# Sparse attention's small matmuls on all 128 rows, with rows of zeros; the sum of squares of the compressed keys as one column

## The chip, the cores and the metric

The kernel runs on one core of one Trainium2 chip. A core has a matrix engine, TensorE (PE), that multiplies a stationary 128x128 array of weights by columns that stream through it and adds into PSUM banks; VectorE (DVE), ScalarE (ACT) and GpSimd (POOL) for everything else; and a queue of transfers issued by SyncE (SP). The metric is the device time of one execution in microseconds (us), lower is better.

## The reference, cut to what matters

Two blocks of two layers each over 256 tokens of width 1024. The change lies in the mixer of the first block, which runs twice (layers 0 and 1). Its sparse attention has 6 heads of 64 in two groups of three; a group shares its keys and values. Three branches are added with gates: compressed, selected and window. With 4 blocks of 64 keys and up to 16 selected, selection takes all that are causal.

```python
k_cmp = rms_norm(compress(kv[0, 0], 0), k_gain[0])     # 15 blocks of 32 tokens, two groups
v_cmp = compress(kv[0, 1], 1)                          # gelu(flat @ cmp_w1[j]) @ cmp_w2[j]
s_c = einsum('bghqd,bgnd->bghqn', qb, k_cmp) + bias_c
o_c = einsum('bghqn,bgnd->bghqd', masked_softmax(s_c, ...), v_cmp)
s_s = einsum('bghqd,bgqkd->bghqk', qb, ks) + bias_s    # selected keys
s_w = einsum('bghqd,bgkd->bghqk', qb, kw) + bias_w     # window keys
return g[..., 0:1] * o_c + g[..., 1:2] * o_s + g[..., 2:3] * o_w
sv = einsum('gts,bcsgd->bctgd', ws * causal, v) + b.T  # spatial gating, also in the mixer
```

## The kernel before, in words

Every large product with weights is made from two halves: a piece of 128x1024 weights is loaded (`raw`, 4 buffers, on SP), ScalarE rounds it to a high half `wh` (line 243), VectorE makes the rest `wl` (line 246), and TensorE adds three products of halves (`mm3`, line 269 records all of `mm1`). Those streams fill most of TensorE's time: `mm<-xx,wh`, `mm<-xx,wl` and so on. A matmul on plain F32 tiles is two passes in the trace; one on F32R tiles is one pass.

In `first_mixer` (twice) the order of each engine's instructions is set when the kernel is built: a list scheduler takes the code in program order, follows the tiles' dependencies and puts other matmuls where one would wait. Each engine then runs its list strictly in order.

What the change touches there:

- `qs`, `ks`, `kl` (lines 688 to 742): queries and keys of the two groups in high and low halves. `qs[:, e]` holds, for group e, the high half of the query on that group's 64 rows and its low half on the other 64. `ks[:, g]` holds the high half of group g's keys on both row halves; so one matmul of 128 rows makes high x high + low x high. `kl` holds the low half of the keys, both groups in one tile, each on its 64 rows, and the second matmul reads those 64 rows alone (line 829 by its code): high x low. Each runs per query tile tt with 2 x 128 or 2 x 256 columns (selected and window keys side by side), per half and per i: 4 x `ks` and 4 x `kl` for each call of `weights(i)`, i from 0 to 2.
- the compressed keys (lines 786 to 815): `gk` and `gv` come out of a gelu; `w2` (64 rows) makes from `gk` the keys and from `gv` the values, three times over, on 96 rows of the bank `kp`. ScalarE squares the keys (`ksq`, 64x32), a matmul with `ones` sums them to 32 rows of `st`, GpSimd raises that to the power -1/2 (`kr`), a matmul with the unit matrix spreads `kr` over all rows (`kb`), and VectorE multiplies (`kcb`). `vblk` (96 rows) is the values masked per group.
- `values(i)`: transposes the weights `z` of the heads (line 856), copies them (`pT`, ScalarE, line 859), multiplies them by the values `vt` (outputs on 64 rows each) and adds the compressed branch: `vblk` and `pcT`, 32 rows per i.
- the spatial gating: `pair` (2 rows) times `gb` (2 rows) puts the bias in the bank, and `vs` by `ws` is added.

`t` is a rotating set of six buffers of 128x256, `z` one of four, `wk` four PSUM banks. SP carries all loads in one list; a load that waits holds those behind it.

Of the kernel before, what the change touches and what calls it, by code (L numbers as in the profile page):

```python
# [1892 lines left out]
```

## Time and profile before

| | us |
|---|---|
| median of 3 runs (1279.09 to 1291.28) | 1288.11 |
| the profiled execution | 1287.02 |
| its span, first to last instruction | 1285.0 |
| TensorE busy | 1258.6 (98%) |
| VectorE busy | 1025.6 (80%) |
| ScalarE busy | 755.3 (59%) |
| GpSimd busy | 35.7 (3%) |

Rows of the timeline give the start, the duration and the instruction; runs of alike instructions are one row with a count (x2), whose duration is that of all of them together. Matmuls overlap in the array, so the distance from one start to the next is what one of them costs, and the duration is longer. In `64*128 64x256` the matmul uses 64 rows and 128 columns of the array, and 256 columns stream through. In square brackets stands what the engine waited for. The granted clock (PEclk) is 1.00 for 2.4 GHz and 0.50 for 1.2 GHz.

### The profile page before, as it was taken

Reading aid. Unit: us, or ns where it says so; the run is one execution under the profiler, and the core shown is the slowest. Engines: PE = TensorE matmul, PEld = TensorE weight load, DVE = VectorE, ACT = ScalarE, POOL = GpSimd, SP = SyncE. Lnnn points to the kernel's source line nnn. Section 1 sums busy time; section 2 is a strip of 40 time slices with the busy share of each in tenths; the row PEclk is TensorE's granted clock in tenths of the full one; section 3 lists DMA queues with packets and bytes.
Section 4 is the critical chain, followed back from the end, with each engine's and each line's share of the span. In section 5 each row is a group of like instructions: output and inputs, shape, how many; then the busy total and the mean of one; then the engine's idle time right before and its main releaser. Section 6 shows DMA issues by size and latency. Waiting matters only on the chain.

```text
span 1285.0 us, 22329 instructions
## 1 busy us (share of the span) xinstructions
PE 1258.6 (98%) x8335; PEld 1125.8 (88%) x8335; DVE 1025.6 (80%) x2294; ACT 755.3 (59%) x1388; POOL 35.7 (3%) x37
## 2 busy tenths in 40 slices
PE   7999999999999999999999999999999999999997
PEld 7887988888998799888889999888888989888886
DVE  6776697776777678998999984899988876999863
ACT  6467376555564846655465553677654565766652
POOL 0000100000010010000000000000000000000000
PEclk9999999999998999999999998999999999999998
DMA  8614456656652346665547242565656443565561
GB/s 285 215 57 133 146 171 191 196 179 187 202 178 72 105 139 214 199 188 184 166 134 240 71 160 60 176 188 189 191 182 193 154 148 116 180 213 187 181 190 34
DMA packets 63313, 211.83 MB, mean 165 GB/s; under 512 B 7992, under 2 KB 10981, under 8 KB 62693
## 3 DMA queue, kind: packets, MB, share of 16 engines
q1 hardware_dynamic: 63204, 210.41, 51.4%
q8 instruction: 65, 1.06, 0.4%
q14 instruction: 44, 0.35, 0.1%
HBM read 209.33 MB, written 1.06 MB: 164 GB/s over the span
## 4 chain that ended last, share of the span: by engine, by line
PE 86%; DVE 7%; ACT 2%; DMA 2%; issue 2%; POOL 0%; SPq 0%; POOLq 0%; DVEq 0%; ACTq 0%
PE mm L269 47%; PE wk L269 37%; DVE wl L246 2%; DMA raw<-weights 1%; ACT wh L243 1%; PE wk L856 1%; DMA z<-bias_line 1%; DMA x<-xt 0%; DVE xx L397 0%; DVE ma L1416 0%; DVE x L345 0%; ACT ks L740 0%; DVE mb L1410 0%; DVE Es L1302 0%; DVE Ec L1301 0%
## 5 line engine op out<-in xcount | busy, mean ns | idle before, releaser
L243 ACT ACTIVATE wh<-raw 128x1024 fp32r<-128x1024 f32 (+3 forms) x394 | 404.9, 1031 | 358.3 <-PE mm L269 164.6
L246 DVE TENSOR_TENSOR wl<-raw,wh 128x512 fp32r<-128x512 f32 (+3 forms) x666 | 500.0, 763 | 141.3 <-ACT wh L243 136.1
L269 PE MATMUL mm<-xx,wh 128*128 128x256 f32 (+1 forms) x1760 | 443.0, 328 | 0.3 <-DVE xx L397 0.3
L269 PE MATMUL mm<-xx,wl 128*128 128x256 f32 x1232 | 348.4, 283 | 1.0 <-DVE wl L246 1.0
L269 PEld LDWEIGHTS mm<-xx,wh 128*128 128x128 f32 x1760 | 297.1, 190 | 31.6 <-issue 2.4
L269 PE MATMUL wk<-xx,wh 128*128 128x512 f32 x704 | 247.6, 392 | 2.5 <-DVE xx L397 2.5
L269 PEld LDWEIGHTS mm<-xx,wl 128*128 128x128 f32 x1232 | 234.3, 190 | 2.0 <-DVE wl L246 1.2
L269 PE MATMUL wk<-xx,wl 128*128 128x256 f32 x704 | 198.5, 282 | 0.0
L269 PEld LDWEIGHTS wk<-xx,wh 128*128 128x128 f32 x704 | 132.2, 188 | 30.5 <-DVE xx L397 1.7
L269 PEld LDWEIGHTS wk<-xx,wl 128*128 128x128 f32 x704 | 133.0, 189 | 0.2
L269 PE MATMUL wk<-aa,wh 128*128 128x512 f32 x352 | 123.0, 392 | 0.0
L269 PE MATMUL mm<-aa,wh 128*128 128x512 f32 x352 | 122.9, 392 | 0.0
L269 PE MATMUL wk<-aa,wl 128*128 128x256 f32 x352 | 98.7, 280 | 0.3 <-DVE wl L246 0.3
L269 PE MATMUL mm<-aa,wl 128*128 128x256 f32 x352 | 98.6, 280 | 0.0
L269 PEld LDWEIGHTS mm<-aa,wh 128*128 128x128 f32 x352 | 66.1, 188 | 14.4
L269 PEld LDWEIGHTS wk<-aa,wh 128*128 128x128 f32 x352 | 66.1, 188 | 14.4
L269 PEld LDWEIGHTS wk<-aa,wl 128*128 128x128 f32 x352 | 66.2, 188 | 0.8 <-DVE wl L246 0.7
L269 PEld LDWEIGHTS mm<-aa,wl 128*128 128x128 f32 x352 | 66.2, 188 | 0.0
L269 PE MATMUL mm<-wh,xx 128*128 128x274 f32 (+3 forms) x224 | 56.0, 331 | 7.4 <-ACT wh L243 7.4
L322 ACT ACTIVATE aa<-a 128x256 fp32r<-128x256 f32 x88 | 35.9, 412 | 23.1 <-DVE a L499 23.1
L269 PEld LDWEIGHTS mm<-wh,xx 128*128 128x128 f32 x224 | 40.0, 199 | 10.4 <-ACT wh L243 7.4
L496 DVE SCALAR_TENSOR_TENSOR e<-gu,par,e 128x255 f32<-128x255 f32 (+1 forms) x88 | 41.3, 475 | 0.0
(476 smaller groups left out, 1779.1 us busy)
## 6 DMA issues: line engine op xcount, KB each, us to landing
raw<-weights SPq DMA_DIRECT2D x344, 512.0 KB, 3.7
raw<-weights SPq DMA_DIRECT2D x46, 384.0 KB, 3.2
h<-w SPq DMA_DIRECT2D x2, 1024.0 KB, 4.8
raw<-weights SPq DMA_DIRECT2D x4, 411.0 KB, 3.9
k_decay<-k_decay SPq DMA_DIRECT2D x1, 1152.0 KB, 7.7
x<-xt SPq DMA_DIRECT2D x4, 256.0 KB, 6.3
h<-s5c SPq DMA_DIRECT2D x1, 1024.0 KB
z<-bias_line SPq DMA_DIRECT2D x2, 384.0 KB, 5.4
```

The lines of the kernel that those rows point to most:

```text
L243: nc.scalar.activation(h[:, :n], r[:, :n], AF.Copy)
L246: self.last_low = nc.vector.tensor_sub(l[:, q], r[:, q], h[:, q].bitcast(F32))
L269: return self.nc.tensor.matmul(out, l, r, start=start, stop=stop, skip_group_check=True)
L322: self.nc.scalar.activation(h, src, AF.Copy)
L496: v.scalar_tensor_tensor(e[:, d:], gu[:, 0, :T - d], col(2 - d), e[:, d:], op0=OP.mult, op1=OP.add)
L856: nc.tensor.transpose(pt[:, blk * 128:blk * 128 + 128], zs[half][:, br, blk * 128:blk * 128 + 128], s.ident)
```

## The change

`kl` gets a dimension for the group; GpSimd clears the rows that are not that group's, once per layer, and the second score matmul reads all 128 rows of `qs` and `kl`. `gk` and `gv` move into one tile `gkv` of 128 rows whose lower half is cleared, and `w2` gets 64 rows of zeros. The matmul for the keys now takes all four of its column blocks (`gk` and three times `gv`). `ksq` squares all 128x128 of it, and the sum over 128 rows counts each square twice, as the keys stand twice in `w2`, hence 1/128 in place of 1/64; it comes out for 128 rows, of which the spread reads 32 through the unit matrix. `vblk` gets one 96x128 block per i, made by a product with the new constant `pick`, which is 1 on the 16 rows of that i and group; the matmul reads 96 rows. `pair` and `gb` get 128 rows with zeros below the second; `gb` moves into one of the `t` buffers, cleared by GpSimd just before its load, and the load is issued later in the program. `u2` takes the tile `turn`, whose use has ended, in place of its own.

```diff
@@ constants
+    pick = np.zeros((128, 3, 2), f)
+    for i in range(3):
+        for g in range(2):
+            pick[32 * i + 16 * g:32 * i + 16 * g + 16, i, g] = 1
+    c["pick"] = pick.reshape(128, 6)
-    pair = np.zeros((2, 128), f)
+    pair = np.zeros((128, 128), f)
@@ first_consts
-    for n in ("m32", "valid", "pair", "tri", "decay"):
+    for n in ("m32", "valid", "pair", "tri", "decay", "pick"):
@@ first_mixer
-    kl = P.tile([128, 2, T], F32R, name="kl")
+    kl = P.tile([128, 2, 2, T], F32R, name="kl")
+    nc.gpsimd.memset(kl[64:128, 0].bitcast(F32), 0.0)
+    nc.gpsimd.memset(kl[0:64, 1].bitcast(F32), 0.0)
...
-                v.tensor_sub(kl[rows[g], i], k[rows[g]], ks[rows[g], g, i].bitcast(F32))
+                v.tensor_sub(kl[rows[g], g, i], k[rows[g]], ks[rows[g], g, i].bitcast(F32))
...
-    w2 = P.tile([64, 192], F32, name="w2")
+    w2 = P.tile([128, 192], F32, name="w2")
...
-    gk = P.tile([64, 32], F32, name="gk")
-    gv = P.tile([64, 3, 32], F32, name="gv")
+    gkv = P.tile([128, 4, 32], F32, name="gk")
+    nc.gpsimd.memset(gkv[64:128], 0.0)
+    gk, gv = gkv[:, 0], gkv[:, 1:4]
...
-    s.mm1(kp[:, 0:32], w2[:, 0:128], gk)
-    s.mm1(kp[0:96, 64:128], gv.rearrange("p i n -> p (i n)"), w2[:, 128:192])
+    s.mm1(kp[:, 0:128], w2[:, 0:128], gkv.rearrange("p i n -> p (i n)"))
+    s.mm1(kp[0:96, 128:192], gv.rearrange("p i n -> p (i n)"), w2[:, 128:192])
...
-    sq = P.tile([64, 32], F32, name="ksq")
-    act(sq, kp[0:64, 0:32], AF.Square)
+    sq = P.tile([128, 128], F32, name="ksq")
+    act(sq, kp[:, 0:128], AF.Square)
...
-    for g in range(2):
-        v.tensor_scalar(vblk[:, g * 64:g * 64 + 64], kp[0:96, 64:128], s.c["cols"][0:96, 4 + g:5 + g], None, op0=OP.mult)
+    vblk = P.tile([96, 3, 2, 64], F32, name="vblk")
+    for i in range(3):
+        v.tensor_mul(vblk[:, i], kp[0:96, None, 128:192].to_broadcast([96, 2, 64]),
+                     s.c["pick"][0:96, 2 * i:2 * i + 2, None].to_broadcast([96, 2, 64]))
...
-    s.mm1(st[0:32, 0:1], sq, s.ones[0:64, 0:1])
+    s.mm1(st[:, 0:1], sq, s.ones[:, 0:1])
...
-    s.mm1(kb[:, 0:32], kr.to_broadcast([32, 128]), s.ident[0:32, 0:32])
+    s.mm1(kb[:, 0:32], kr.to_broadcast([128, 128]), s.ident[:, 0:32])
...
-                s.mm1(S[:, :2 * n], q[r], kl[r, :, :n], False, True)
+                s.mm1(S[:, :2 * n], q, kl[:, half, :, :n], False, True)
...
-        y = s.mm1(o[:, 0:T], vblk[q, :], pcT[q, :], False, True)
+        y = s.mm1(o[:, 0:T], vblk[:, i].rearrange("p a b -> p (a b)"), pcT, False, True)
...
-    gb = P.tile([2, 2, 128], F32, name="gb")
-    s.dma(gb, s.ext(f"gb{l}", ...))
...
-    u2 = P.tile([128, 2, T], F32, name="u2")
+    u2 = turn
...
+    gb = tmp().rearrange("p (a b) -> p a b", a=2)
+    nc.gpsimd.memset(gb, 0.0)
+    s.dma(gb[0:2], s.ext(f"gb{l}", ...))
...
-        f = s.mm1(o[:, 0:T], s.c["pair"], gb[:, i, None, :].to_broadcast([2, 2, 128]), True, False)
+        f = s.mm1(o[:, 0:T], s.c["pair"], gb[:, i, None, :].to_broadcast([128, 2, 128]), True, False)
```

The scheduler orders anew what follows. On TensorE, at the first scores of layer 0 (`kr` is the reciprocal root of the compressed keys, `kcb` the scaled compressed keys), before:

```order
L269 MATMUL wk<-k_ident,kr 128x32
L269 MATMUL wk<-ks,qs 128x256
L269 MATMUL wk<-kl,qs 128x256
L269 MATMUL wk<-ks,qs 128x512
L269 MATMUL wk<-kl,qs 128x512
L269 MATMUL wk<-ks,qs 128x256
L269 MATMUL wk<-kl,qs 128x256
L269 MATMUL wk<-ks,qs 128x512
L269 MATMUL wk<-kl,qs 128x512
L269 MATMUL wk<-kcb,qh 128x32 x6
```

and in the changed kernel:

```order
L275 MATMUL wk<-k_ident,kr 128x32
L275 MATMUL wk<-ks,qs 128x256
L275 MATMUL wk<-kl,qs 128x256
L275 MATMUL wk<-ks,qs 128x512
L275 MATMUL wk<-kl,qs 128x512
L275 MATMUL wk<-ks,qs 128x256
L275 MATMUL wk<-kl,qs 128x256
L275 MATMUL mm<-xx,wl 128x256
L275 MATMUL mm<-wh,xx 128x384
L275 MATMUL mm<-wl,xx 128x384
L275 MATMUL wk<-ks,qs 128x512
L275 MATMUL wk<-kl,qs 128x512
L275 MATMUL wk<-kcb,qh 128x32 x6
```

Three matmuls of the stream stand between the third and the fourth pair. On TensorE in layer 1, around the matmul that reads `gk`, before:

```order
L269 MATMUL mm<-xx,wh 128x256
L269 MATMUL wk<-gk,w_4170 128x32
L269 MATMUL wk<-w_4170,gv 96x64
L269 MATMUL mm<-xx,wh 128x256
L269 MATMUL mm<-xx,wl 128x256
L269 MATMUL mm<-xx,wh 128x256
L269 MATMUL wk<-ones,ksq 32x1
```

and now:

```order
L275 MATMUL mm<-xx,wh 128x256 x2
L275 MATMUL wk<-gk,w_4177 128x128
L275 MATMUL wk<-w_4177,gk 96x64
L275 MATMUL mm<-xx,wl 128x256
L275 MATMUL mm<-xx,wh 128x256 x2
L275 MATMUL mm<-xx,wl 128x256
L275 MATMUL wk<-ones,ksq 128x1
```

One stream matmul more stands ahead of `gk`, one more ahead of `ksq`, and three more (10 in place of 7) between `ksq` and `kr`. On GpSimd in layer 0 (`rrr` is the reciprocal root of a retention head pair, `t` here is `gb`):

```order
L360 TENSOR_TENSOR rrr<-rvv,mhalf 128x4
L1029 MEMSET t 128x256
L360 TENSOR_TENSOR rrr<-rvv,mhalf 128x4
L360 TENSOR_TENSOR r_1532<-v_1531,mhalf 128x8
L360 TENSOR_TENSOR rrr<-rvv,mhalf 128x4
```

The memset is new between the first two. On SP in layer 0 the load of `gb` stood right behind that of `ws`, and now:

```order
L180 DMA ws<-ws 128x512
L180 DMA raw<-weights 128x1024 x15
L180 DMA t<-gb 2x256
L180 DMA raw<-weights 128x1024 x44
```

It has moved behind 15 pieces of weights.

## Rows read from the trace of the kernel before

**Rows 1.** The page, part 1: busy time and share of the span
```profile
PE 1258.6 (98%) x8335; PEld 1125.8 (88%) x8335; DVE 1025.6 (80%) x2294; ACT 755.3 (59%) x1388; POOL 35.7 (3%) x37
```

**Rows 2.** Waits of TensorE: total us, times, longest us
```profile
PE wk L269 <- DMA z<-bias_line: 2.6, 2, 2.0
...
PE wk L269 <- issue: 1.5, 2, 1.2
```

**Rows 3.** Timeline of TensorE, layer 1: start us, us, instruction, [idle before]
```profile
393.24 0.38 PE L269 MATMUL wk<-gk,w 64*128 64x32 f32 x2 [1.18 <-issue]
...
395.79 0.58 PE L269 MATMUL wk<-ks,qs 128*128 128x256 f32 x1
...
400.72 2.77 PE L269 MATMUL wk<-kcb,qh 128*128 128x32 f32 x12
```

**Rows 4.** Timeline of TensorE, layer 0: stream, then the first scores
```profile
69.20 0.40 PE L269 MATMUL mm<-xx,wh 128*128 128x256 f32 x2
...
69.55 0.40 PE L269 MATMUL mm<-xx,wh 128*128 128x256 f32 x2
...
70.32 0.38 PE L269 MATMUL wk<-ks,qs 128*128 128x256 f32 x1
70.64 0.38 PE L269 MATMUL wk<-kl,qs 64*128 64x256 f32 x1
70.95 0.49 PE L269 MATMUL wk<-ks,qs 128*128 128x512 f32 x1
71.37 0.50 PE L269 MATMUL wk<-kl,qs 64*128 64x512 f32 x1
...
73.28 1.52 PE L269 MATMUL wk<-kcb,qh 128*128 128x32 f32 x12
```

**Rows 5.** Timeline of TensorE, feed-forward of layer 0: stream of 512 and 256 columns
```profile
200.08 0.39 PE L269 MATMUL wk<-xx,wh 128*128 128x512 f32 x1
...
200.42 0.39 PE L269 MATMUL wk<-xx,wh 128*128 128x512 f32 x1
```

**Rows 6.** Windows: stretch, length, busy us (x instructions) per engine, PEclk, DMA
```profile
70.30:74.90 4.60, 4.60 (x23) 3.10 (x23) 3.66 (x8) 2.30 (x9) 0.00 (x0) 1.00 0.01 4
74.90:78.30 3.40, 3.40 (x18) 3.40 (x18) 3.27 (x12) 3.31 (x12) 0.00 (x0) 0.50 0.00 0
...
395.70:406.00 10.30, 10.30 (x34) 7.61 (x34) 6.81 (x19) 5.79 (x18) 0.00 (x0) 0.50 0.07 27
```

**Rows 7.** Timeline of TensorE, layer 0: compressed values, then the bias by `pair`
```profile
98.58 0.69 PE L269 MATMUL wk<-pcT,vblk 32*128 32x256 f32 x2
99.21 0.38 PE L269 MATMUL wk<-kl,qs 64*128 64x256 f32 x1
...
139.05 1.13 PE L269 MATMUL wk<-gb,k_pair 2*128 2x256 f32 x4
140.11 0.38 PE L269 MATMUL mm<-mixh,wh 128*128 128x256 f32 x1
```

**Rows 8.** Timeline of VectorE, layer 1, around `gk` and `vblk`
```profile
392.10 0.94 DVE L246 TENSOR_TENSOR wl<-raw,wh 128x768 fp32r<-128x768 f32 x1
392.97 0.17 DVE L790 TENSOR_SCALAR gk<-e 64x32 f32<-64x32 f32 x1
...
394.18 0.46 DVE L803 TENSOR_SCALAR vblk<-wk,k_cols 96x64 f32<-96x64 f32 x2
```

**Rows 9.** Timeline of GpSimd, layer 0
```profile
0.73 0.26 POOL L622 MEMSET cb<- 128x192 f32 x1 [0.29 <-POOLq L1887]
...
117.82 1.94 POOL L354 TENSOR_TENSOR rrr<-rvv,mhalf 128x4 f32<-128x4 f32 x1 [48.15 <-DVE rvv L926]
```

**Rows 10.** Timeline of ScalarE and TensorE, layer 0, at the first `pT`
```profile
89.84 0.49 ACT L859 ACTIVATE pT<-wk 128x384 f32<-128x384 f32 x1 [2.55 <-PE wk L856]
...
90.41 0.43 PE L269 MATMUL wk<-pT,vt 128*64 128x256 f32 x1
```

**Rows 11.** Windows of the densest attention: columns as in rows 6, ScalarE the fourth
```profile
93.00:106.00 13.00, 13.00 (x89) 10.11 (x86) 10.01 (x22) 11.71 (x41) 0.00 (x0) 1.00 0.38 118
...
418.00:431.00 13.00, 13.00 (x75) 9.35 (x74) 10.73 (x25) 11.84 (x45) 0.00 (x0) 1.00 0.12 34
```

More of the change, by code (lines that the diff above doesn't have):

```diff
@@ L754, in first_mixer @@
     s.dma(ka[:, :, 32:34, :], s.ext(f"pe{l}", pe))
-    w2 = P.tile([64, 192], F32, name="w2")
+    w2 = P.tile([128, 192], F32, name="w2")
     c2 = np.asarray(inp["cmp_w2"][l])
-    s.dma(w2, s.ext(f"w2_{l}", np.concatenate([c2[0], c2[0], c2[1]], 1)))
+    c2 = np.concatenate([c2[0], c2[0], c2[1]], 1)
+    s.dma(w2, s.ext(f"w2_{l}", np.concatenate([c2, np.zeros_like(c2)], 0)))
     w1 = s.act.tile([128, 2, 8, 128], F32, name="h")
@@ L787, in first_mixer @@
     gelu2(s, e1, e0, *(P.tile([64, 2, 32], F32, name="cg", bufs=2) for _ in range(2)))
-    gk = P.tile([64, 32], F32, name="gk")
-    gv = P.tile([64, 3, 32], F32, name="gv")
-    v.tensor_scalar(gk, e1[:, 0, :], 0.5, None, op0=OP.mult)
-    v.tensor_scalar(gv, e1[:, 1:2, :].to_broadcast([64, 3, 32]), 0.5, None, op0=OP.mult)
+    gkv = P.tile([128, 4, 32], F32, name="gk")
+    nc.gpsimd.memset(gkv[64:128], 0.0)
+    gk, gv = gkv[:, 0], gkv[:, 1:4]
+    v.tensor_scalar(gk[0:64], e1[:, 0, :], 0.5, None, op0=OP.mult)
@@ L792, in first_mixer @@
+    v.tensor_scalar(gv[0:64], e1[:, 1:2, :].to_broadcast([64, 3, 32]), 0.5, None, op0=OP.mult)
     kp = s.bank("wk")
-    s.mm1(kp[:, 0:32], w2[:, 0:128], gk)
-    s.mm1(kp[0:96, 64:128], gv.rearrange("p i n -> p (i n)"), w2[:, 128:192])
+    s.mm1(kp[:, 0:128], w2[:, 0:128], gkv.rearrange("p i n -> p (i n)"))
+    s.mm1(kp[0:96, 128:192], gv.rearrange("p i n -> p (i n)"), w2[:, 128:192])
     gm = P.tile([128, 32], F32, name="gm")
     v.tensor_scalar(gm, s.c["m32"], s.P[f"kc{l}"], None, op0=OP.mult)
-    sq = P.tile([64, 32], F32, name="ksq")
@@ L798, in first_mixer @@
-    act(sq, kp[0:64, 0:32], AF.Square)
+    sq = P.tile([128, 128], F32, name="ksq")
+    act(sq, kp[:, 0:128], AF.Square)
     kcs = P.tile([128, 32], F32, name="kcs")
     v.tensor_mul(kcs, kp[:, 0:32], gm)
-    vblk = P.tile([96, 128], F32, name="vblk")
-    for g in range(2):
-        v.tensor_scalar(vblk[:, g * 64:g * 64 + 64], kp[0:96, 64:128], s.c["cols"][0:96, 4 + g:5 + g], None, op0=OP.mult)
+    vblk = P.tile([96, 3, 2, 64], F32, name="vblk")
+    for i in range(3):
+        v.tensor_mul(vblk[:, i], kp[0:96, None, 128:192].to_broadcast([96, 2, 64]),
+                     s.c["pick"][0:96, 2 * i:2 * i + 2, None].to_broadcast([96, 2, 64]))
@@ L804, in first_mixer @@
     st = s.bank("wk")
-    s.mm1(st[0:32, 0:1], sq, s.ones[0:64, 0:1])
-    kv = P.tile([32, 1], F32, name="kv")
-    kr = P.tile([32, 1], F32, name="kr")
-    v.tensor_scalar(kv, st[0:32, 0:1], 1.0 / 64, EPS, op0=OP.mult, op1=OP.add)
+    s.mm1(st[:, 0:1], sq, s.ones[:, 0:1])
+    kv = P.tile([128, 1], F32, name="kv")
+    kr = P.tile([128, 1], F32, name="kr")
+    v.tensor_scalar(kv, st[:, 0:1], 1.0 / 128, EPS, op0=OP.mult, op1=OP.add)
     s.rsqrt(kr, kv)
     kb = s.bank("wk")
-    s.mm1(kb[:, 0:32], kr.to_broadcast([32, 128]), s.ident[0:32, 0:32])
+    s.mm1(kb[:, 0:32], kr.to_broadcast([128, 128]), s.ident[:, 0:32])
@@ L822, in weights @@
             z = P.tile([128, 2, 384], F32, name="z", bufs=4)
-            r = rows[half]
             for tt in range(2):
@@ L1018, in first_mixer @@
     v.tensor_mul(vs, v28, r8[:, :, None].to_broadcast([128, 8, 64]))
+    gb = tmp().rearrange("p (a b) -> p a b", a=2)
+    nc.gpsimd.memset(gb, 0.0)
+    s.dma(gb[0:2], s.ext(f"gb{l}", np.asarray(inp["gm_b"][l]).reshape(2, 2, 128).transpose(1, 0, 2)))
     o2 = ret_a(2)
```

2 lines of the change are left out of this document (removed).

## The prediction

> **What bounds the kernel now.** I read the page's busy shares first: TensorE 1258.6 of 1285.0 us, VectorE 80%, ScalarE 59% [rows 1]. So time goes only where TensorE's own stream gets shorter. Next the waits of TensorE: of its 26.4 us without work, 2.6 us are for the bias tables of layer 0, and 1.5 us, put down to nothing in particular, are in the code of this change [rows 2]; 1.18 of them stand in layer 1 before the matmul that reads `gk` [rows 3]. Then the timeline of TensorE, in which the starts say more than the durations, since matmuls overlap: the ends are modelled, and a busy TensorE is not one at its peak.
>
> In a stream of full-array matmuls a 256-column one follows the next after 0.117 us: three starts between 69.20 and 69.55 [rows 4]. A 512-column one takes 0.223 us: the pair 512 + 256 recurs every 0.34 us, less 0.117 [rows 5]. In the sparse attention the same sizes, alternating between 128 rows (`ks`) and 64 rows (`kl`), start 0.31 us (256) and 0.42 us (512) apart [rows 4]: about 0.2 us more at each change of the row count, in both directions, although no wait stands in those rows.
>
> Last the granted clock by stretches [rows 6]. It is at the 1.2 GHz level (0.50) from 74.9 to 78.3 us, behind 4.6 us in which TensorE was busy throughout with this alternating sequence and the short `kcb` matmuls; and from 395.7 to 406.0 us, behind the stretch with the 1.18 us wait and the 64- and 32-row matmuls of the compressed keys.
>
> **The change, part by part.**
>
> Low halves of the keys. `kl` becomes two tiles with the other group's rows zero; its 24 matmuls (two layers, three values of i, two halves, two row tiles) use all rows, so neither the 24 entries nor the 24 exits change the shape. They stand in six groups of four `ks` and four `kl`. The group at 70.32 takes until 73.28 us, 2.96 us [rows 4]; in a stream it takes 4 x 0.117 + 4 x 0.223 = 1.36. That is 1.60 us each, **9.6 us** for six at full clock. What it can't be more than is this, since the columns stay.
>
> Compressed values. Six products of `pcT` (32 rows, two passes each) take 0.63 us from their start to the start of what follows [rows 7]; two passes in a stream take 0.23. The entry stays dear, since the 64-column `pT` matmuls stand in front before and after. 0.40 x 6 = **2.4 us**.
>
> `pair`. Two products of four passes together take 1.06 us [rows 7] per layer against 4 x 0.117 = 0.47: 0.59 a layer. In layer 0 of the changed order the two products stand apart, with 64-column matmuls between, which adds two changes of shape at about 0.15 us. 1.18 - 0.3 = **0.9 us**.
>
> `gk`, `gv`, `ksq`, `kr`: some eight entries and exits in both layers, between nothing and 0.2 us each by the `kl` rows, so 0 to 1.6 us; but the moving side of the first grows from 32 to 128 columns and the weights of the third from 32 to 128 columns. I take **0.5 us**, nearer the low end.
>
> One rule of the Trainium skill speaks against the change. Its page "TensorE: Matmul & The Clock Gate", Part 3, says that matmuls on few rows should be kept on separate row groups, because such matmuls run concurrently. By it the 24 `kl` matmuls would be free beside others now, and filling them with zeros would cost their whole stream time. The rows say otherwise: each `kl` starts 0.31 to 0.43 us behind its neighbour, since the neighbours use all rows and no second row group stands beside it [rows 4]. The sum goes by the rows.
>
> Clock. At 0.50 half of the time is lost: (3.4 + 10.3) / 2 = **6.8 us** if both stretches come back. Sizes agree with the rows: the first group of layer 1 takes 4.93 us (395.79 to 400.72) where the one of layer 0 took 2.96 [rows 3, 4]. Nothing lost is the other end. I take the whole, because both falls stand behind part-filled matmuls which the change fills, and what preceded the first was no idle time at all [rows 6].
>
> What is added. VectorE writes `vblk` in three instructions of 96x128 with two tensors in place of two of 96x64 (0.46 us together [rows 8]): between nothing more and, if each costs by its columns, 3 x 2 x 0.23 = 1.38, so up to 0.9 us more a layer; half of it is my value, 0.4. It delays `kv`, `kr` and the `kr` matmul; the changed order puts about three more stream matmuls (0.35 us) ahead of that matmul in layer 1, which is the cover; without it TensorE waits that 0.4 us in each layer. ScalarE's `ksq` grows from 64x32 to 128x128: a fraction of a microsecond, under the same cover. GpSimd clears `kl`, `gkv` and `gb`: the nearest row is 0.26 us for 128x192, and `rrr` itself takes 1.94 [rows 9]. The first two are long done before use; that of `gb` stands between the first and the second `rrr`, behind 117.82 + 1.94 = 119.76 us, so it is hidden as long as a buffer `t` comes free. The load of `gb` moves behind 15 weight pieces on the SP queue and waits for that memset; the `pair` product that needs that needs it stood at 139.05 [rows 7], 19 us behind the end of the first `rrr`.. Cost taken: nothing. `pick` is one more small load ahead of the bias tables, for whose return TensorE waits: between nothing and one issue slot on SP; I take 0.3 us.
>
> Waits that come up. TensorE reaches its consumers earlier. They have little spare: `pT` at 89.84 lasts 0.49 and ends at 90.33, and the matmul that reads it starts at 90.41 [rows 10]. ScalarE is busy 11.71 of 13 us and 11.84 of 13 us in the two densest stretches [rows 11]. The list scheduler has put other matmuls in between, and outside these stretches ScalarE has room. The bounds are nothing and about 8 us (the share of the gain that lies in those stretches and the ones beside them). I take 1.7 us. The wait for `gk` stays: it ends on VectorE, behind a `wl` of 0.94 us [rows 8], and the order there is the same.
>
> **Sum.** 9.6 + 2.4 + 0.9 + 0.5 + 6.8 = 20.2 us gained, 0.3 + 1.7 = 2.0 given back: 18.2. The profiled execution took 1287.0 us (span 1285.0 and 2.0 around it), 1.1 below the median of 1288.1 of the runs shown, so it is a typical one. 1287.0 - 18.2 = 1268.8, so **1269 us**.
>
> **The rivals.**
>
> *The clock stays low in layer 1.* For it: the 1.18 us wait stays, the compressed keys are still a run of tiny matmuls, and the stretch was the longer of the two. [...] Against it: the fall of layer 0 had no gap ahead [rows 6]. Time: only 1.7 of the 6.8 us come back, 1268.8 + 5.1 = 1274.
>
> *The attention becomes bound by ScalarE.* For it: 11.71 and 11.84 of 13 us and `pT` just in time [rows 10, 11]. Then of the 12 us of `kl` and `pcT` only about half are kept, and the clock half comes back too: 1287 - 6 - 1.4 - 3.4 + 0.3 = 1276 to 1281.
>
> *Slower.* GpSimd's clearing of `gb` needs a free `t` buffer of six, and `gb` now holds one until the end of the mixer. `rrr` of the second head pair stands behind it on GpSimd, its `rrx`, `ret_c` and the last output products behind that, and the load of `gb` with all weight pieces behind it on SP. It decides if TensorE stands still for more than the gain, 9 us a layer; from the end of the first `rrr` to the `pair` products there are 19 us in which the order has other work. Time with 15 us a layer: 1268.8 + 30 = 1299 and above. The other way to be slower, the rule on row groups, is worth 12 x 0.117 + 12 x 0.223 = 4.1 us at most: 1291.
>
> *No change in the hardware's cost*, because what costs 0.2 us is the change of weights and not that of shape: against it stands the stream itself, which changes weights at every matmul and keeps 0.117 us. Time 1287 - 1.
>
> **How the numbers follow.** Forecast 0.55. Clock stays low in layer 1: 0.17. ScalarE bound: 0.21. Rule on row groups or no effect: 0.04. Slower through GpSimd and SP: 0.03. The range takes in the forecast with half-clock stretches elsewhere falling differently (the runs before spread from 1279 to 1291 without any change), hence 1259 at the low end, and the first two rivals, hence 1282. A difference of 1% (below 1275.2 or above 1301) is about what a measurement of this kernel can tell from no change. Faster by over 1%: the forecast, most of the first rival and none of the second, 0.68; within 1%: 0.29; slower: 0.03.
>
> **What would show it.** Timeline: `ks` and `kl` starting about 0.12 and 0.22 us apart, `pcT` passes 0.12 apart. Windows: granted clock 1.00 through both sparse stretches. Waits of TensorE: few new ones on ScalarE's `pT` and `z`; total idle time below 29 us (26.4 before). Wrong it would be if the starts stay 0.3 us apart, if the clock falls again at the compressed keys, or if the busy time of TensorE falls while its idle time takes up the difference.

## The result and the profile after

The changed kernel takes 1272.8 us (median of 7 runs, 1269.56 to 1274.96) against 1284.97 (7 runs, 1279.09 to 1291.28): a ratio of 0.9899, interval 0.9873 to 0.9925. Measured again beside other kernels it was 1273.08 against 1286.34, 0.9902 (0.9871 to 0.9933). The forecast was 1269, its range 1259 to 1282. The profiled execution took 1272.23 us, 14.8 less than that of the kernel before.

Line numbers have moved by 6 to 12: L269 is L275 now, L246 is L252, L354 is L360. The busy times, as in [rows 1], page of the changed kernel:

```profile
PE 1244.1 (98%) x8335; PEld 1122.9 (88%) x8335; DVE 1025.8 (81%) x2296; ACT 754.4 (59%) x1388; POOL 39.1 (3%) x45
```

TensorE lost 14.5 us of busy time, and its idle time is what it was: 1270.5 - 1244.1 = 26.4, as 1285.0 - 1258.6 before. The windows show where. Two mixers of the kernel before (from the first matmul of the compression to the first of the feed-forward; TensorE's busy time is the second figure, PEclk the third from the end):

```profile
59.20:161.30 102.10, 101.47 (x716) 86.77 (x714) 69.64 (x157) 58.91 (x143) 6.18 (x5) 0.98 0.37 117
383.70:491.50 107.80, 106.32 (x742) 91.04 (x740) 73.16 (x165) 60.11 (x142) 7.26 (x7) 0.95 0.36 112
```

The same two stretches of the changed kernel, and the two stretches at half clock that it has outside them:

```profile
58.50:153.50 95.00, 93.39 (x711) 84.40 (x710) 69.42 (x158) 58.25 (x143) 6.89 (x6) 1.00 0.38 126
377.00:476.10 99.10, 97.64 (x742) 88.12 (x741) 72.79 (x166) 59.47 (x142) 7.55 (x8) 1.00 0.39 122
641.60:645.00 3.40, 3.40 (x12) 2.92 (x12) 3.40 (x14) 3.20 (x12) 0.00 (x0) 0.50 0.02 6
689.40:696.20 6.80, 6.80 (x33) 6.58 (x32) 6.80 (x17) 0.64 (x2) 0.00 (x0) 0.50 0.30 91
```

The mixers are 7.1 and 8.7 us shorter, 15.8 together, of which 6.8 is the half of the stretches of [rows 6], both gone. About 1.1 us is given back behind the first mixer (below), and 0.9 behind the second.

The first scores of layer 0, as in [rows 4]. Timeline of TensorE, changed kernel:

```profile
72.12 0.41 PE L275 MATMUL wk<-k_ident,kr 128*128 128x32 f32 x2 [1.09 <-POOL kr L360]
72.37 0.36 PE L275 MATMUL wk<-ks,qs 128*128 128x256 f32 x1
72.57 0.28 PE L275 MATMUL wk<-kl,qs 128*128 128x256 f32 x1
72.69 0.40 PE L275 MATMUL wk<-ks,qs 128*128 128x512 f32 x1
72.92 0.40 PE L275 MATMUL wk<-kl,qs 128*128 128x512 f32 x1
...
386.58 0.46 PE L275 MATMUL wk<-gk,w 128*128 128x128 f32 x2 [1.09 <-issue]
...
389.30 0.36 PE L275 MATMUL wk<-ks,qs 128*128 128x256 f32 x1
...
390.78 1.46 PE L275 MATMUL wk<-kcb,qh 128*128 128x32 f32 x12
```

`kl` starts 0.20 us behind the first `ks`, and from there the starts are 0.12 and 0.23 us apart, where 0.31 and 0.42 stood. In layer 1 the wait ahead of `gk` has stayed (1.09, 1.18 in [rows 3]), and yet the first group takes 1.48 us (389.30 to 390.78) in place of 4.93. New is the 1.09 us wait for `kr` in the first row. Two waits of TensorE from the list of the changed kernel, and the row in which the bias products start:

```profile
PE wk L275 <- issue: 2.8, 2, 1.7
...
PE wk L275 <- POOL kr L360: 1.1, 1, 1.1
```

```profile
55.66 2.98 PE L275 MATMUL wk<-z,t 128*128 128x512 f32 x8 [1.69 <-issue]
```

The 2.8 us are the 1.09 ahead of `gk` and 1.69 ahead of the bias products, where 2.6 stood in the kernel before [rows 2]. No line of the list names `pT` or `z`: ScalarE has not become the bound.

### The profile page after: what moved, and what is told of

It reads as the page before. It is cut to its first block, busy times and chain, and to the rows that moved or that the text cites. A ratio compares the mean times of both kernels' runs of the same rounds, so it can differ in the third digit from the quotient of the medians.

```text
span 1270.5 us, 22337 instructions
## 1 busy us (share of the span) xinstructions
PE 1244.1 (98%) x8335; PEld 1122.9 (88%) x8335; DVE 1025.8 (81%) x2296; ACT 754.4 (59%) x1388; POOL 39.1 (3%) x45
## 3 DMA queue, kind: packets, MB, share of 16 engines
q8 instruction: 65, 1.06, 0.3%
HBM read 209.49 MB, written 1.06 MB: 166 GB/s over the span
## 4 chain that ended last, share of the span: by engine, by line
PE 92%; DVE 2%; DMA 2%; ACT 1%; issue 1%; POOL 0%; SPq 0%; POOLq 0%; DVEq 0%; ACTq 0%
PE mm L275 52%; PE wk L275 39%; DMA raw<-weights 2%; DVE wl L252 1%; PE wk L868 1%; ACT wh L249 1%; DVE x L351 0%; PE wk L1778 0%; DVE xx L450 0%; SPq L180 0%; ACT z L1768 0%; POOL kr L360 0%; DVE Ec L1313 0%; DVE Es L1314 0%; DVE xx L403 0%
## 5 line engine op out<-in xcount | busy, mean ns | idle before, releaser
L252 DVE TENSOR_TENSOR wl<-raw,wh 128x512 fp32r<-128x512 f32 (+3 forms) x666 | 500.9, 764 | 137.7 <-ACT wh L249 132.8
L275 PE MATMUL mm<-xx,wh 128*128 128x256 f32 (+1 forms) x1760 | 441.1, 327 | 0.4 <-DVE xx L403 0.4
L275 PE MATMUL mm<-xx,wl 128*128 128x256 f32 x1232 | 347.7, 282 | 0.6 <-DVE wl L252 0.5
L275 PEld LDWEIGHTS mm<-xx,wh 128*128 128x128 f32 x1760 | 295.9, 189 | 30.5 <-issue 1.5
L275 PE MATMUL wk<-xx,wh 128*128 128x512 f32 x704 | 247.6, 392 | 2.5 <-DVE xx L403 2.5
L275 PEld LDWEIGHTS mm<-xx,wl 128*128 128x128 f32 x1232 | 233.5, 189 | 1.7 <-DVE wl L252 0.9
L275 PE MATMUL wk<-xx,wl 128*128 128x256 f32 x704 | 198.4, 282 | 0.0
L275 PEld LDWEIGHTS wk<-xx,wh 128*128 128x128 f32 x704 | 132.2, 188 | 30.5 <-DVE xx L403 1.7
L275 PEld LDWEIGHTS wk<-xx,wl 128*128 128x128 f32 x704 | 133.0, 189 | 0.2
L275 PE MATMUL mm<-aa,wh 128*128 128x512 f32 x352 | 125.0, 397 | 0.0
L275 PE MATMUL wk<-aa,wh 128*128 128x512 f32 x352 | 123.5, 393 | 0.0
L275 PE MATMUL mm<-aa,wl 128*128 128x256 f32 x352 | 99.4, 282 | 0.0
L275 PE MATMUL wk<-aa,wl 128*128 128x256 f32 x352 | 98.7, 280 | 0.0
L275 PEld LDWEIGHTS mm<-aa,wh 128*128 128x128 f32 x352 | 66.8, 190 | 15.2
L275 PEld LDWEIGHTS wk<-aa,wh 128*128 128x128 f32 x352 | 66.1, 188 | 14.9
L275 PEld LDWEIGHTS mm<-aa,wl 128*128 128x128 f32 x352 | 67.0, 190 | 0.0
L275 PEld LDWEIGHTS wk<-aa,wl 128*128 128x128 f32 x352 | 66.2, 188 | 0.1
L275 PE MATMUL mm<-wh,xx 128*128 128x274 f32 (+3 forms) x224 | 54.9, 329 | 7.3 <-ACT wh L249 7.3
L275 PEld LDWEIGHTS mm<-wh,xx 128*128 128x128 f32 x224 | 39.9, 199 | 8.9 <-ACT wh L249 7.3
```

What stands on the lines that cost most here:

```text
L252: self.last_low = nc.vector.tensor_sub(l[:, q], r[:, q], h[:, q].bitcast(F32))
L275: return self.nc.tensor.matmul(out, l, r, start=start, stop=stop, skip_group_check=True)
```

## Two numbers for each kernel

The stretches at half clock fall in other places from one execution to the next, so the time of a run mixes two things. Each run lists its span and its mean granted clock. Their product says how long the span would be at full clock throughout; the rest is what half clock cost. Half clock at the start of the program, where TensorE waits for weights anyway, is counted as a loss too: it lasts 11.2 to 13.9 us in the profiled executions, so about 6 us of each rest are the start's. The clock is listed to 0.001, which is 1.3 us of the span, so a single product is good to about 1 us.

| kernel | runs | median us | span x clock, mean us | rest, mean us (lowest to highest) |
|---|---|---|---|---|
| before | 38 | 1284.9 to 1286.4 | 1268.2 | 15.3 (7.7 to 24.5) |
| changed | 13 | 1272.8 and 1273.1 | 1260.8 | 10.3 (5.1 to 17.9) |
| all_but_kl | 10 | 1286.95 | 1269.2 | 16.9 |
| two_by_two | 8 | 1280.4 | 1266.3 | 12.8 |
| kl_alone_2 | 4 | 1272.69 | 1259.8 | 11.4 |
| kr_and_place | 4 | 1269.97 | 1261.9 | 7.0 |
| old_values | 2 | 1272.92, 1273.91 | 1259.7, 1263.2 | 11.4, 8.9 |
| old_pair | 1 | 1269.26 | 1261.2 | 6.3 |
| late_vblk | 9 | 1266.51 and 1270.24 | 1256.7 | 10.1 |
| place_64 | 1 | 1269.59 | 1258.9 | 8.9 |

So the change is worth 7.4 us by its structure and 5.0 by the clock. The 5.0 is a mean: the rests of both kernels overlap.

For parts of the change a third figure is read from the traces: the distance from each matmul's start to the next start, less what its columns take in a stream (0.117 us for 256, 0.222 for 512, 0.109 for 128 or fewer), stretches at half clock counted by half, summed over both mixers and over all steps that begin or end at a matmul of that part. It is called the excess below. It is read as a difference between kernels; a step between two parts counts for both.

## The experiments

**Is the gain that of kl, and whose is the clock?** The change without `kl`, then `kl` without the change.

```diff
-    kl = P.tile([128, 2, 2, T], F32R, name="kl")
-    nc.gpsimd.memset(kl[64:128, 0].bitcast(F32), 0.0)
-    nc.gpsimd.memset(kl[0:64, 1].bitcast(F32), 0.0)
+    kl = P.tile([128, 2, T], F32R, name="kl")
...
-                s.mm1(S[:, :2 * n], q, kl[:, half, :, :n], False, True)
+                s.mm1(S[:, :2 * n], q[r], kl[r, :, :n], False, True)
```

> The changed kernel with kl back in one tile and its matmuls on 64 rows; everything else of the change stays. Theory A: the kl starts are 0.31 and 0.42 us apart again, both half-clock stretches of the sparse attention return, and what is left of the change is about 1 us gained at pcT and 2.2 lost (wait for kr 1.1, matmuls of aa 1.1): about 1 us above the kernel before, 1286 against 1285. Theory B (layer 1's fall belongs to the compressed keys): the stretch of layer 0 returns, that of layer 1 does not, so about 4 us below the kernel before, 1281. The other rival, that the six groups are worth the forecast 9.6 us, would put it 2.3 us higher than either.

1286.95 us, ratio to the kernel before 1.0021 (0.9986 to 1.0056). Theory A's 1286 holds, B's 1281 does not: without `kl` nothing is gained, at full clock or by the clock. Windows of its two mixers, and two of the stretches at half clock in them:

```profile
60.20:164.30 104.10, 102.46 (x712) 88.99 (x710) 69.61 (x158) 58.98 (x143) 6.91 (x6) 0.95 0.37 116
387.70:493.50 105.80, 105.49 (x742) 92.21 (x740) 72.98 (x166) 60.05 (x142) 7.56 (x8) 0.97 0.36 114
```

```profile
76.60:83.40 6.80, 6.80 (x25) 5.82 (x24) 5.36 (x17) 1.86 (x8) 0.00 (x0) 0.50 0.00 0
...
390.60:397.40 6.80, 6.80 (x34) 6.80 (x33) 5.30 (x16) 1.24 (x5) 0.00 (x0) 0.50 0.28 82
```

The clock is below 1.00 in both. In layer 0 the stretch of [rows 6] is back, behind the first scores (`kl` from 74.33 us). In layer 1 it is not: half clock there ends at 397.4 us, ahead of `gk` (399.26) and of the first scores (401.98). The theories differ on the stretch of layer 1 too, and there this trace does not bear out theory A. The excess of `kl` is 9.2 us here, 8.8 in the kernel before, 1.1 in the changed one.

The other way round, on the kernel before. `u2` takes the tile `turn` as in the changed kernel: with a tile of its own the mixer needs 87.8 KB of each partition, and 86.4 are free.

```diff
-    kl = P.tile([128, 2, T], F32R, name="kl")
+    kl = P.tile([128, 2, 2, T], F32R, name="kl")
+    nc.gpsimd.memset(kl[64:128, 0].bitcast(F32), 0.0)
+    nc.gpsimd.memset(kl[0:64, 1].bitcast(F32), 0.0)
...
-                s.mm1(S[:, :2 * n], q[r], kl[r, :, :n], False, True)
+                s.mm1(S[:, :2 * n], q, kl[:, half, :, :n], False, True)
...
-    u2 = P.tile([128, 2, T], F32, name="u2")
+    u2 = turn
```

> The kernel before with only the low halves of the keys (kl) on 128 rows, and u2 in the tile turn to make room. all_but_kl put the rest of the change at a loss of 1 us with the clock taken out (span times mean granted clock: 1269.2 against 1268.2 for the kernel before and 1260.8 for the changed one). Theory A (the two parts add up, kl is the whole gain): span times clock comes to 1268.2 - 8.4 = 1259.8, no wait for kr in layer 0, the aa matmuls 0.229 us apart, the time lost to half clock 10 us as in the changed kernel (15 before), total 1271.6, about 1 us below the changed kernel. Theory B (kl and the other row fillings help only together, for instance because pcT and kl stand beside each other and share their changes of shape): span times clock stays above 1262 and the total above 1274.

1272.69 us, 0.9905 (0.9871 to 0.994); span x clock 1259.8, the number of theory A, and 11.4 lost to the clock. `kl` alone is as fast as the whole change: what the other parts gain, side costs of the change take again. The clock is not cured by it in every execution; the profiled one still has 0.98 in both mixers. In layer 0 half clock stands ahead of the first scores (`kl` from 75.05 us), in layer 1 it begins 1.7 us behind the wait for `gk`:

```profile
61.90:160.00 98.10, 97.48 (x715) 86.39 (x714) 68.52 (x156) 57.64 (x141) 6.17 (x5) 0.98 0.37 118
382.30:482.60 100.30, 98.83 (x743) 88.42 (x741) 72.65 (x165) 59.92 (x142) 7.29 (x7) 0.98 0.40 120
```

```profile
391.78 0.38 PE L269 MATMUL wk<-gk,w 64*128 64x32 f32 x2 [1.13 <-issue]
```

```profile
393.50:396.90 3.40, 3.40 (x14) 2.92 (x14) 1.39 (x4) 2.12 (x2) 0.36 (x1) 0.50 0.42 154
```

**Is it the change of shape that costs, or the 64 rows?** The kernel before, its row counts as they were, in an order with half the changes; each product keeps its bank.

```diff
+            Ss = []
...
                 s.mm1(S[:, :2 * n], q, ks[:, half, :, :n], True, False)
+                Ss.append(S)
+            for tt in range(2):
+                n = 128 + 128 * tt
+                S = Ss[tt]
+                q = qs[:, half, i, tt * 128:tt * 128 + 128]
                 s.mm1(S[:, :2 * n], q[r], kl[r, :, :n], False, True)
```

> The kernel before with the score matmuls of a half in another order: ks 256, ks 512, kl 256, kl 512, in place of ks, kl, ks, kl. Row counts and columns are as before, only the changes of row count are halved: 4 in place of 8 in the first group with its exit. Theory A (each change of shape costs about 0.2 us): the first group of layer 0 takes 1.36 + 4 x 0.2 = 2.2 us in place of 2.96, and all six groups give about half of 7.3, 3.5 to 4 us. Rival (64-row matmuls are slow by themselves, or change of weights is what costs): the group stays at 2.9 to 3.0 us. The time of the kernel: about 1281 by A if the stretches at half clock stay, 1275 if they go too, 1285 by the rival.

Timeline of TensorE, the first group (each row is a 256- and a 512-column matmul):

```profile
72.62 0.62 PE L269 MATMUL wk<-ks,qs 128*128 128x256 f32 x2
73.17 0.62 PE L269 MATMUL wk<-kl,qs 64*128 64x256 f32 x2
73.72 0.61 PE L269 MATMUL wk<-ks,qs 128*128 128x256 f32 x2
74.26 0.61 PE L269 MATMUL wk<-kl,qs 64*128 64x256 f32 x2
74.80 1.52 PE L269 MATMUL wk<-kcb,qh 128*128 128x32 f32 x12
```

2.18 us where 2.2 was expected by the price per change and 2.9 to 3.0 by the rival; a pair takes 0.55, 0.2 above the 0.34 of a stream, whether on 64 rows or on 128. The excess of `kl` falls from 8.8 to 5.0. So the price belongs to the change of shape, not to the 64 rows. The whole kernel: 1280.4, 0.9971 (0.9933 to 1.0008), too near to 1 to say more. By span x clock it gains 1.9 us, half of the 3.8 by the excess; where the other half went is not shown.

**What holds kr, and why is the feed-forward slower?** In the changed kernel the power for `kr` takes 1.80 us in layer 0, 0.59 before. And the 352 matmuls that read `aa` in the first feed-forward, which the change does not touch, take 62.05 us from the first start to the last, 60.91 before. No wait stands there. What has changed is the place of `aa` in SBUF as the program lays it out: `pick` ahead of it moves it from byte 140896 of each partition to 140928. Two edits of the changed kernel:

```diff
-    pick = np.zeros((128, 3, 2), f)
+    pick = np.zeros((128, 8, 2), f)
...
+    nc.gpsimd.memset(kr, 0.0)
-    s.rsqrt(kr, kv)
+    s.rsqrt(kr[0:32], kv[0:32])
```

> The changed kernel with two things mended. One: GpSimd raises only 32 rows of kv to the power, into a kr tile of 128 rows cleared once beforehand. Two: the constant pick gets 16 columns in place of 6 (the added ones zero), so that the tiles behind it, aa of the first feed-forward among them, lie 32 bytes past a multiple of 64 again as in the kernel before, and not on one. On the first, theory A (a one-off price of about 1.2 us falls on the first short power on all 128 rows of a run): kr takes 0.6 us, the wait of TensorE for kr in layer 0 (1.09 us) goes, and the first rrr takes 1.9 us again as in the kernel before, hidden. Rival (the form 128x1 itself is slow, or the place in the run): rrr stays at 1.0, or kr stays at 1.8. On the second, theory A (the place of aa costs): its 512-column matmuls start 0.229 us apart in place of 0.235, so 1.1 us less between the first and the last of them. Rival: they stay at 0.235. Together 2.2 us below the changed kernel: 1270.6 against 1272.8.

The time, 1269.97 us (0.988, 0.9819 to 0.9942), is near the 1270.6 expected, but by the clock (7.0 us lost, 10.3 in the changed kernel); the rows show that neither edit did its work. VectorE's rows around the power in that kernel:

```profile
71.94 0.41 DVE L585 TENSOR_TENSOR t<-t 128x256 f32<-128x256 f32 x1
72.27 1.22 DVE L252 TENSOR_TENSOR wl<-raw,wh 128x1024 fp32r<-128x1024 f32 x1
```

and GpSimd's:

```profile
72.17 1.73 POOL L360 TENSOR_TENSOR kr<-kv,mhalf 32x1 f32<-32x1 f32 x1 [22.38 <-DVE kv L822]
116.43 1.01 POOL L360 TENSOR_TENSOR rrr<-rvv,mhalf 128x4 f32<-128x4 f32 x1 [42.54 <-DVE rvv L938]
```

`kr` takes 1.73 us on 32 rows as well, and `rrr` stays at 1.01; so it is neither the 128 rows nor a one-off that moves on. The power ends at 73.90, 0.41 us behind the end of `wl` (72.27 + 1.22 = 73.49). In the changed kernel it ends at 72.07, 0.41 behind `wl`:

```profile
70.05 0.14 DVE L821 TENSOR_SCALAR kv<-wk 128x1 f32<-128x1 f32 x1
70.12 0.41 DVE L585 TENSOR_TENSOR t<-t 128x256 f32<-128x256 f32 x1
70.45 1.21 DVE L252 TENSOR_TENSOR wl<-raw,wh 128x1024 fp32r<-128x1024 f32 x1
```

In the kernel before VectorE had products with one SBUF tile behind `kv`, and `kr` took 0.59 us. But `rrr` at 117.82 took 1.94 us [rows 9], 1.01 elsewhere, and there a `wl` ran:

```profile
68.86 0.13 DVE L808 TENSOR_SCALAR kv<-wk 32x1 f32<-32x1 f32 x1
68.93 0.59 DVE L888 TENSOR_SCALAR rk<-t,k_cols 128x256 f32<-128x256 f32 x2
...
117.66 1.22 DVE L246 TENSOR_TENSOR wl<-raw,wh 128x1024 fp32r<-128x1024 f32 x1
```

The new theory: GpSimd's power stands still while VectorE works on two SBUF tiles, if VectorE was first. The Trainium skill says this in "SBUF — State Buffer", section "Who interferes with whom": a VectorE instruction with two SBUF inputs contends with a GpSimd instruction that reads SBUF, the shared ports are an exclusive lock, and the order of issue decides who is blocked. These rows agree, with VectorE first: 1.80 and 1.73 us in place of 0.59, both ending 0.41 behind `wl`.

On `aa`: 62.06 us again at 140960, so 32 past a multiple of 128 is as dear as 0; the kernel before had 96.

**The mend of both.** The `vblk` products, which read PSUM and the small `pick`, move behind the power in program order, and `pick` gets 32 columns (`aa` at 96 past a multiple of 128). On the changed kernel:

```diff
-    pick = np.zeros((128, 3, 2), f)
+    pick = np.zeros((128, 16, 2), f)
...
-    vblk = P.tile([96, 3, 2, 64], F32, name="vblk")
-    for i in range(3):
...
     st = s.bank("wk")
...
     s.rsqrt(kr, kv)
+    vblk = P.tile([96, 3, 2, 64], F32, name="vblk")
+    for i in range(3):
...
```

> The changed kernel with the three vblk products moved behind the power that makes kr, and with pick at 32 columns in place of 6 (the added ones zero), so that aa of the first feed-forward lies 96 bytes past a multiple of 128 as in the kernel before (0 past it in the changed kernel, 32 in kr_and_place). On kr, theory A (GpSimd's power stands still while VectorE runs a product of two SBUF tiles, here wl of 1.21 us right behind kv): VectorE now has three products of 0.2 us with one side in PSUM behind kv, so kr takes 0.55 us in place of 1.80, and TensorE's wait of 1.09 us for kr goes. Rival (the place in the run, or a slow first power of this kind): kr stays at 1.7 to 1.8 us. On aa, theory A (the place modulo 128 costs): 0.229 us apart again, 1 us less between the first and the last. Rival (any move of aa, or the size of the pool before it): 0.234. Together 2.1 us below the changed kernel's 1272.8 at equal clock.

VectorE, and then GpSimd, in that kernel:

```profile
69.64 0.16 DVE L817 TENSOR_SCALAR kv<-wk 128x1 f32<-128x1 f32 x1
69.72 0.67 DVE L821 TENSOR_TENSOR vblk<-wk,k_pick 96x128 f32<-96x128 f32 x3
```

```profile
69.88 0.55 POOL L360 TENSOR_TENSOR kr<-kv,mhalf 128x1 f32<-128x1 f32 x1 [21.77 <-DVE kv L817]
```

`kr` takes 0.55 us, and TensorE waits 0.31 for it, and 0.19 in layer 1 where it did not wait. The `aa` matmuls take 60.90. The durations of their 512-column ones (busy us, mean ns of one), first in the changed kernel and as well in `kr_and_place`, then in this kernel, each over the stretch of that product:

```profile
L275 PE MATMUL mm<-aa,wh 128*128 128x512 f32 x88 | 31.3, 397 | 0.0
```

```profile
L275 PE MATMUL mm<-aa,wh 128*128 128x512 f32 x88 | 30.7, 390 | 0.0
```

1266.51 us, 0.9861 (0.9828 to 0.9895) of the kernel before. To see how much of that is the clock, both kernels once more on one chip:

> The changed kernel itself, beside the one with its two side costs mended, on the same chip: 1272 to 1273 us, 1% below the kernel before; span times mean granted clock 1260.8, the loss at half clock 10 us.

> The kernel of late_vblk once more. If its gain over the changed kernel belongs to the structure (no wait for kr, aa at its old place modulo 128, and an order with less idle time), span times clock is 3.5 to 4 us below that of the changed kernel on the same chip and the median 4 to 7 us below it, 1266 to 1268. If the four runs before were lucky with the clock, the medians are within 3 us of each other.

1273.08 and 1270.24 us (0.9874 of before, 0.985 to 0.9899). Span x clock is 1260.8 and 1256.5: the structure's 4.3 us are there again, a little above the forecast. The medians differ by 2.8 only, not by 4 to 7, since this time half clock cost the mended kernel 11.7 and the changed one 10.4. Of the 4.3 us, 1.15 are those of `aa` and 0.6 those of `kr`; the rest, about 2.5, stands for the most part in the new order of the mixers (the excess of `pair` is 0.59 in place of 1.16, that of `ks` 0.96 in place of 1.67) and belongs to neither mend by anything shown. By span x clock the mended kernel is the best of the study.

**Where exactly is aa's bad place, and is the port a race?** On late_vblk:

```diff
-    pick = np.zeros((128, 16, 2), f)
+    pick = np.zeros((128, 12, 2), f)
```

> The kernel of late_vblk with pick at 24 columns in place of 32: aa of the first feed-forward lies 64 bytes past a multiple of 128 (96 in late_vblk and in the kernel before, 0 in the changed kernel, 32 in kr_and_place). If the place modulo 128 counts and 96 is the good one, its 352 matmuls take about 62 us from the first start to the last, as at 0 and 32; if only the lower half of each 128 bytes is dear, 60.9 as at 96. The wait for kr stays away in both.

60.90 us, as at 96. So an `aa` at 0 or 32 past a multiple of 128 costs 1.15 us over 352 matmuls, one at 64 or 96 nothing. Why is not known; the weights `wh` and `wl`, which the same matmuls read, lie at the same bytes in all these kernels.

The changed kernel with the compressed values as before:

```diff
-    vblk = P.tile([96, 3, 2, 64], F32, name="vblk")
+    vblk = P.tile([96, 128], F32, name="vblk")
...
-        y = s.mm1(o[:, 0:T], vblk[:, i].rearrange("p a b -> p (a b)"), pcT, False, True)
+        q = slice(32 * i, 32 * i + 32)
+        y = s.mm1(o[:, 0:T], vblk[q, :], pcT[q, :], False, True)
```

> The changed kernel with the compressed values as before: vblk of 96x128, its matmul on the 32 rows of each i. By the forecast the change of this part is worth 0.4 us per product, 2.4 us in all: the two passes would stand 0.31 us apart now and 0.12 in the changed kernel. By the trace of the changed kernel it is worth about 0.15 each, 0.9 in all, because the first step after the entry from 64-column matmuls is 0.32 us on 96 rows too. So here: passes 0.31 to 0.32 apart as well, the exit to a 128-row matmul 0.31 in place of 0.2 or less, the mixers 0.9 us longer (0.4 and 0.5).

Timeline of TensorE, layer 0, here:

```profile
97.00 0.69 PE L275 MATMUL wk<-pcT,vblk 32*128 32x256 f32 x2
97.63 0.39 PE L275 MATMUL wk<-ks,qs 128*128 128x256 f32 x1
```

and in the changed kernel:

```profile
96.14 0.70 PE L275 MATMUL wk<-pcT,vblk 96*128 96x256 f32 x2
96.49 0.47 PE L275 MATMUL wk<-kl,qs 128*128 128x256 f32 x1
96.80 0.40 PE L275 MATMUL wk<-ks,qs 128*128 128x512 f32 x1
```

0.63 us from `pcT` to what follows on 32 rows, 0.35 on 96 rows, but then the `kl` behind it takes 0.31 in place of 0.12. The excess of `pcT` is 2.9 here and 1.85 in the changed kernel: 1.05 us for six, near the 0.9 that the trace of the changed kernel gave and far from 2.4. Nor did this kernel lose time by it: 1272.92, for it had no wait for `kr`. GpSimd:

```profile
72.75 0.66 POOL L360 TENSOR_TENSOR kr<-kv,mhalf 128x1 f32<-128x1 f32 x1 [24.69 <-DVE kv L820]
```

VectorE's order behind `kv` is that of the changed kernel:

```profile
72.59 0.41 DVE L585 TENSOR_TENSOR t<-t 128x256 f32<-128x256 f32 x1
72.92 1.21 DVE L252 TENSOR_TENSOR wl<-raw,wh 128x1024 fp32r<-128x1024 f32 x1
```

The power ends at 73.41, 0.41 us behind the end of `t` (73.00), while `wl` runs. So `t` held it here, and `wl` did not. The same kernel again:

> The kernel of old_values once more, for one question: there the power for kr took 0.66 us although wl came right behind kv as in the changed kernel, where it took 1.80 in two executions out of two. If the order of arrival at a shared port decides and it is a close one, kr may take 1.80 us this time, ending 0.41 us after wl, with a wait of TensorE of about 1.1 us; if something fixed in this kernel keeps kr clear of wl, it takes 0.66 again.

```profile
71.62 1.80 POOL L360 TENSOR_TENSOR kr<-kv,mhalf 128x1 f32<-128x1 f32 x1 [22.08 <-DVE kv L820]
```

1.80 this time, with TensorE waiting 1.1 us: the same program, once clear and once held. That fits a close race between the power and `wl` for the port as `t` ends, and no fixed property of the kernel. The race itself is not seen in a row, and no row shows `wl` held in its turn: it takes 1.21 us in the execution that the power won.

**Pair**, on the changed kernel:

```diff
-    pair = np.zeros((128, 128), f)
+    pair = np.zeros((2, 128), f)
...
-    nc.gpsimd.memset(gb, 0.0)
...
-        f = s.mm1(o[:, 0:T], s.c["pair"], gb[:, i, None, :].to_broadcast([128, 2, 128]), True, False)
+        f = s.mm1(o[:, 0:T], s.c["pair"], gb[0:2, i, None, :].to_broadcast([2, 2, 128]), True, False)
```

> The changed kernel with pair and gb on 2 rows again and without the clearing of gb by GpSimd; gb stays in its t buffer and at its place on SP. By the forecast filling the rows is worth 0.45 us a layer, 0.9 in all. By the trace of the changed kernel next to nothing, since pair stands between 64-column matmuls whose entries and exits stay: within 0.1 us a layer. GpSimd loses the 0.32 us memset in each layer, which by both nobody waited for.

The excess of `pair` is 1.61 us here and 1.16 in the changed kernel: 0.45 for both layers, above the 0.1 a layer that the trace suggested and half of the forecast. Two of its products in a row, on full rows (changed kernel, layer 1):

```profile
453.92 1.11 PE L275 MATMUL wk<-t,k_pair 128*128 128x256 f32 x4
454.68 0.47 PE L275 MATMUL mm<-mixh,wh 128*128 128x256 f32 x1
```

take 0.76 us where 1.06 stood, in layer 0 [rows 7] and in layer 1. Where they stand apart between 64-column matmuls, as in layer 0, little is left of that. Nobody waited for the memset, in either kernel.

## Why the prediction was right, and by how much its terms were off

| term | forecast us | measured us | from |
|---|---|---|---|
| `kl` | 9.6 | 7.6 | excess 8.75 to 1.13; 8.4 by span x clock against all_but_kl |
| `pcT` | 2.4 | 1.05 | excess 2.90 to 1.85 |
| `pair` | 0.9 | 0.2 to 0.45 | excess 1.32 before, 1.61 in old_pair, 1.16 now |
| `gk` and the rest of the keys | 0.5 | 0.3, not clear of noise | excess of `gk` and `gv` 1.93 to 1.59, the wait in it included |
| clock | 6.8 | 6.8 in the profiled pair, 5.0 over all runs | windows; 15.3 to 10.3 |
| bias line | -0.3 | 0.9 in the profiled pair | wait ahead of the bias products 2.58 to 1.69 |
| new waits | -1.7 | -1.05 | excess of `kr` 0.39 to 1.43; none on ScalarE |
| place of `aa` | not named | -1.15 | 60.91 to 62.05 us |

**Low halves of the keys.** The mechanism holds: starts 0.12 and 0.23 us apart, and two_by_two ties the price to the change of shape. The size was read from the densest group and set to 0.2 us for 48 changes; over all six groups they cost 8.75, 0.18 each, and 1.13 of it stays: a group that stands behind another shape still pays its entry, and a 512-column step takes 0.233, not 0.223. The rule of the Trainium skill that was weighed against the change ("TensorE: Matmul & The Clock Gate", Part 3, on row groups) does not bear on these matmuls: kl_alone_2 fills them with zeros and gains 8.4 us.

**Keys.** The 0.3 us of `gk` are not a measure of the filling: most of that excess is the wait ahead of `gk`, which comes and goes between executions of one program (0.62 and 1.67 in the two of `late_vblk`).

**Compressed values and pair.** The step that failed is "two passes in a stream take 0.23", and for `pair` "4 x 0.117". 0.117 us is the step of the F32R stream. `vblk`, `pcT`, `pair` and `gb` are plain F32, and 256-column passes on plain F32 tiles step 0.216 us on the full array too (the median of 29 steps between passes of `u` and `raw` in the second block). Eight of them, with the exit, take 1.79 us (kernel before):

```profile
790.94 1.89 PE L269 MATMUL wk<-u,raw 128*128 128x256 f32 x8
792.73 0.74 PE L269 MATMUL mm<-xx,wh 128*128 128x256 f32 x4
```

At that price two passes take 0.43, the most to be had is 0.63 - 0.43 = 0.20 for each of the six products, 1.2 in all, and 1.06 - 0.86 = 0.20 a layer for `pair`. 1.05 were measured for the six, and 0.2 to 0.45 for `pair` in both layers. The entry from 64-column matmuls stays (0.32 between the two passes of `pcT`, in both kernels), so the sign "`pcT` passes 0.12 apart" did not come; the exit gets shorter, and the step behind it longer.

**Clock.** The forecast took both stretches whole and chose so because the first had no idle time ahead of it. In both profiled executions of the changed kernel just that came out, with a wait of 1.09 and 1.22 us for `gk` still there, so the rival (the wait stays, layer 1 stays low, 1274) is out for these executions. But the kernel before loses between 7.7 and 24.5 us to half clock from run to run; one profile is one draw, and the mean gain is 5.0. By the means it is `kl` that brings this: 16.9 us are lost without it and 11.4 with it alone, over 10 and 4 runs.

Which filling takes which stretch away is not shown, and the traces do not give both to `kl`. In layer 0 half clock begins within 5 us of the first scores in the two kernels that alternate `ks` and 64-row `kl` (at 74.9 and 76.6 us) and in none of the eleven other traces. In layer 1 it begins within 3 us behind the wait for `gk` in the two traces that have this wait and the compressed keys on 64 rows, the kernel before and `kl_alone_2`, and in none of the six that have the wait and these keys on full rows; so there the compressed keys may be what counts. Further stretches, in kernels with and without the filling, stand ahead of the scores (at 61.6 us in `late_vblk_again`, at 390.6 in `all_but_kl`).

**New waits.** The amount was near, the cause was not. ScalarE was feared and is in no wait; GpSimd came instead. The step on what is added asked how much longer VectorE's `vblk` makes the way to `kr` (0.4 us) and what covers that; it did not ask what the new order puts behind `kv`: `t` and `wl`, both products of two SBUF tiles, where the kernel before had `rk`. The memset and load of `gb` were hidden as said.

**Sum.** 18.2 was forecast, 14.8 measured between the profiled executions, 12.2 to 13.3 between the medians. The terms above give 7.6 + 1.05 + 0.2 + 0.3 + 6.8 + 0.9 - 1.05 - 1.15 = 14.65 for the profiled pair. That it is so near is partly chance: the mixers are 0.9 us shorter than their terms say, and what follows the second mixer is 0.9 us longer in the changed kernel (794.4 against 793.5). The forecast of the time, 1269, is nearer (3.8 us) than that of the gain (5 to 6), and this is luck: it starts from an execution of 1287.0 us, taken as typical from three runs, where the medians of the larger groups of runs are 1284.9 to 1286.3.

## What to carry to other kernels

In a stream of full-array matmuls count the changes of shape, not the small matmuls: each cost 0.18 us here, zeros in the unused rows take most of it away if the neighbours have the full shape too, and grouping equal shapes took 3.8 of 8.8 us of the excess away without any zeros. Price a pass by the type of its tiles: 256 columns step 0.117 us in the F32R stream here and 0.216 on plain F32 tiles. When a chain goes VectorE, GpSimd, TensorE, look at what VectorE runs right behind the first link: a product of two SBUF tiles may hold GpSimd for its whole length, and moving three small PSUM reads there cut the waits for `kr` from 1.09 to 0.50 us. A new constant moves every tile behind it; compare untouched code by first and last start.
